# Where the first three chunks of gated activations are split: from PSUM, or after a round trip through DRAM

## The chip, the cores and the metric

The kernel runs on one core of one Trainium2 chip. The metric is the device time of one execution in microseconds (us); lower is better. TensorE is called PE here, VectorE DVE, ScalarE ACT, GpSimd POOL and SyncE SP, as in the profile.

## The reference

One decoder layer on 256 tokens of width 2048. The first half (three attention mixers, their projections, gates and an output projection) is not touched by the change. The second half is a SwiGLU feed-forward layer in float32:

```python
    h2 = rmsnorm(x, g_ffn)
    gu = h2 @ w_gu                                    # 256 x 2048 times 2048 x 11264
    x = x + (jax.nn.silu(gu[..., :D_FF]) * gu[..., D_FF:]) @ w_down   # D_FF = 5632
```

## The kernel before

**Precision.** Every float32 matrix is taken apart into two `fp32r` parts, `hi` (a cast by ACT) and `lo` (source minus `hi`, a subtraction by DVE), by `split` (lines 103 to 107; its two instructions stand at line 105 in the profile). A product is three matmuls, hi·hi, hi·lo and lo·hi (`product`, lines 167 to 169). The left operand, the activations, is loaded as 128x128 weights; the weight matrix streams as 512 columns. So PE needs, for each 128x1024 block of weights that SP fetches, one ACT cast (`w_hi`) and one DVE subtraction (`w_lo`). `w_hi` and `w_lo` have 5 buffers each, the raw blocks 4 to 6.

**The gate and up stage.** A loop over 11 chunks `c` of 512 columns of D_FF. Each turn calls `project_pair`, which computes the gate and the up columns of one chunk together by a Strassen-like scheme (fewer products, more additions on DVE, and two accumulating DMAs on POOL, `u<-g_raw` at line 360). It ends with Silu (ACT, line 947) and a multiplication (DVE, line 948), which leave two 128x512 tiles `sg`, one for each half `t` of the tokens. For the down projection these must be transposed; `to_a` is queued in `stages` and advanced between the weight blocks of the next `project_pair`, so the transposes of chunk `c` run early in the turn of chunk `c+1`.

**`to_a`.** `transpose4` makes four 128x128 transposes on PE (line 189) into one PSUM bank, a `tr` tile (2 buffers). ACT copies it to SBUF (line 938), and POOL issues a DMA that writes it to `a_mem` in DRAM (line 939).

**`take_a`.** It reads a whole chunk back from `a_mem` with a DMA on POOL (line 959) into `a_raw` (2 buffers) and splits it into the chunk's place in the object `a` (tiles `a_hi`, `a_lo`, and others for the chunks in `WD`). For the three chunks 0, 1 and 2 (`ORDER[:EARLY]`) the place is in the pool `pe`, which is free during the gate and up stage; for the other eight it is in `pd`, whose memory is the normed activations `h2` until that stage ends.

**What sets the order.** The program is written once and a scheduler orders each engine's queue by its own estimate of when things become ready. Each engine then runs its queue strictly in that order: an instruction that waits holds up all that stand behind it on its engine. The scheduler put the splits of chunks 0 to 2 into the gate and up stage, one in each of the turns 1, 2 and 3.

Of the kernel before, what the change touches and what calls it, by code (L numbers as in the profile page):

```python
# [27 lines left out]
NF = D_FF // P  # L28
# [26 lines left out]
def hybrid_block(ctx: ExitStack, tc: tile.TileContext, x, g_mix, w_in, q_gain, k_gain, w_branch, w_out,  # L55
# [22 lines left out]
    def pool(stack, name, side, bufs=1):  # L78
        return stack.enter_context(tc.tile_pool(name=name, bufs=bufs, side=side, reuse_waits="tile"))
# [8 lines left out]
    def half_kb(dt=F32):  # L88

        return scratch.tile([P, NB], dt, name="sc")  # L90
# [13 lines left out]
    def split(hi, lo, src, pin=False):  # L104
        for op in nc.scalar.copy(hi, src), nc.vector.tensor_sub(lo, src, hi.bitcast(F32)):  # L105
            if pin:
                tc.keep_in_program_order(op)
# [77 lines left out]
    def transpose4(src):  # L185

        pt = tr.tile([P, 4, P], F32, name="tr")
        for i in range(4):
            nc.tensor.transpose(pt[:, i, :], src[:, i * P:(i + 1) * P], ident)  # L189
        return pt  # L190
# [696 lines left out]
    pe = pool(ctx, "pe", "left")  # L887
# [43 lines left out]

    a_mem = dram.tile([NF // 4, P, 4, S], F32, name="a_mem")

    def to_a(c, srcs):
        for t in range(NT):
            pt = transpose4(srcs[t])
            st = half_kb().rearrange("p (k q) -> p k q", k=4)
            nc.scalar.copy(st, pt)
            nc.gpsimd.dma_start(a_mem[c, :, :, t * P:(t + 1) * P], st)
            yield  # L940

    for c in range(D_FF // NB):
        nxt = (h2, w_gu, (c + 1) * NB, D_FF + (c + 1) * NB) if c + 1 < D_FF // NB else None
        (g0, g1_, u0, u1), ahead = project_pair(h2, w_gu, c * NB, D_FF + c * NB, ahead, nxt)
        sg = [half_kb() for _ in range(NT)]
        for t, (g, u) in enumerate(((g0, u0), (g1_, u1))):
            nc.scalar.activation(sg[t], g, AF.Silu, scale=rstd2[:, t:t + 1])
            nc.vector.scalar_tensor_tensor(sg[t], u, rstd2[:, t:t + 1], sg[t], op0=ALU.mult, op1=ALU.mult)
        stages.append(to_a(c, sg))

    WD = (4, 6, 8)
    ORDER = [0, 1, 2, 4, 3, 6, 5, 8, 7, 9, 10]
    EARLY = 3
    a = Chunks(None, "a", NF // 4, WD, False)

    def take_a(pl, c):
        a.place(pl, c)
        raw = pr.tile([P, 4, S], F32, name="a_raw", bufs=2)
        nc.gpsimd.dma_start(raw, a_mem[c])
        if c in WD:  # L960
            t0, t1 = (raw[:, :, t * P:(t + 1) * P] for t in range(NT))
            a.put(c, 0, t0)
            a.put(c, 1, t1)
            a.put_sums(c, t0, t1, raw)
        else:
            split(*a.t[c], raw)

    for c in ORDER[:EARLY]:
        take_a(pe, c)
    h2_stack.close()  # L970
    pd = pool(ctx, "pd", "left")

    def take_rest():
        for c in ORDER[EARLY:]:
            take_a(pd, c)
            yield
            yield
# [3 lines left out]
    def down_pair(c0, mine, spare, queues):  # L981
# [25 lines left out]
        def seven(c, f1, f5, f6, f7, last):  # L1007
            def quarter(kh, n):
                return load(w_down, 4 * c + 2 * kh, c0 + n * NB, gd)

            b11 = quarter(0, 0)
            form(f1, 1, c, b11, last)
            yield
            b12 = quarter(0, 1)
            u = gd.tile([P, 2, NB], F32, name="u", bufs=1)
            tc.keep_in_program_order(nc.vector.tensor_add(u, b11, b12))
            form(f5, 5, c, u, last)
            yield
            b22 = quarter(1, 1)
            nc.vector.tensor_add(u, u, b22)  # L1020
            form(f6, 6, c, u, last)
            yield
            nc.vector.tensor_add(b12, b12, b22)
            form(f7, 7, c, b12, last)
            yield
            form(own[0, 1], 3, c, b22)
            yield
            b21 = quarter(1, 0)
            form(own[0, 0], 2, c, b21)
            yield  # L1030
            nc.vector.tensor_add(u, u, b21)
            form(own[1, 0], 4, c, u)
            yield

        def combine(f1, f5, f6, f7):

            s1 = snapshot(f1)
            nc.vector.tensor_add(xc[0, 0], xc[0, 0], s1)
            nc.vector.tensor_add(s1, f6, s1)
            s3 = half_kb()  # L1040
            nc.vector.tensor_add(s3, f7, s1)
            s5 = snapshot(f5)
            yield
            nc.vector.tensor_add(xc[1, 0], xc[1, 0], s3)
            nc.vector.tensor_sub(s1, s5, s1)
            nc.vector.tensor_add(xc[0, 1], xc[0, 1], s1)
            nc.vector.tensor_sub(s3, s5, s3)
            nc.vector.tensor_add(xc[1, 1], xc[1, 1], s3)
            yield

        def by_sevens():
            f = spare()
            for c in WD:
                yield from seven(c, *f, c == WD[-1])
            yield from combine(*f)

        sevens = by_sevens()
        plain = [(c, n, kh) for c in ORDER if c not in WD for kh in range(2) for n in range(2)]
        for i, at in enumerate(plain[:-4]):
# [56 lines left out]
```

## Time and profile before

| | |
|---|---|
| median of 3 runs | 1387.82 us (1387.64 to 1389.24) |
| profiled execution, own time | 1387.56 us |
| span in its profile | 1385.8 us |
| PE busy | 1362.3 us, 98% |
| DVE busy | 1151.7 us, 83% |
| ACT busy | 880.9 us, 64% |
| POOL busy | 109.4 us, 8% |
| mean granted PE clock | 0.994 |
| DMA | 331.07 MB, mean 239 GB/s |

The gate and up stage reaches from about 700 us to 1144 us of the span, the down projection from there to the end. In the rows that follow, "idle before <- releaser" in brackets is how long the engine stood still before an instruction and what came last. `DMA_DIRECT2D` is the issue of a DMA, not its transfer. A number after `x` counts merged instructions. `PEld` is the load of weights on PE. The names `ps`, `qs`, `z` and `v` are the PSUM accumulators, `tr` the transposed tiles, `h_shi` and `h_slo` the summed activations of the scheme.

### The profile page before, as it was taken

What the parts mean: (1) busy time and instruction counts of PE and PEld (TensorE: products, weight loads), DVE (VectorE), ACT (ScalarE), POOL (GpSimd) and SP (SyncE); (2) the same over time, 40 slices, a digit from 0 to 9 for tenths busy, and PEclk for the clock granted to TensorE, in tenths of its full rate; (3) what the DMA queues carried; (4) which work ended last, traced back from release to release, by engine and by line L of the source; (5) the groups of instructions that cost most, each with busy time, mean ns of one, the idle gap of its engine ahead of it and who ended that gap; (6) DMA issues with size and microseconds to landing.
All of it is one profiled execution on the core that took longest, in us unless ns stands there. A gap on an engine that the chain in (4) does not pass through costs nothing.

```text
span 1385.8 us, 17910 instructions
## 1 busy us (share of the span) xinstructions
PE 1362.3 (98%) x6404; PEld 1184.9 (85%) x6404; DVE 1151.7 (83%) x1222; ACT 880.9 (64%) x1140; POOL 109.4 (8%) x173
## 2 busy tenths in 40 slices
PE   9999999999999999999999988999999999999998
PEld 7888888888888888888887877888888888788887
DVE  7888797858989987776698877999999998887785
ACT  7678877767776665445565656667666665564553
POOL 1100000000010112101001001010000010100000
PEclk9999999999999999999999999999999999999999
DMA  8875567576687779877887677678787877767553
GB/s 277 288 255 169 202 181 257 147 242 196 244 286 266 263 228 336 276 220 227 294 276 252 224 244 228 214 259 285 247 277 244 274 216 236 258 239 258 195 178 101
DMA packets 93928, 331.07 MB, mean 239 GB/s; under 512 B 11312, under 2 KB 12928, under 8 KB 93840
## 3 DMA queue, kind: packets, MB, share of 16 engines
q1 hardware_dynamic: 76896, 275.29, 57.1%
q0 software_dynamic: 15760, 53.60, 15.0%
q8 instruction: 50, 0.82, 0.2%
q10 hardware_dynamic: 1184, 1.06, 0.2%
q14 instruction: 38, 0.31, 0.1%
HBM read 292.65 MB, written 16.27 MB: 223 GB/s over the span
## 4 chain that ended last, share of the span: by engine, by line
PE 77%; issue 12%; DMA 4%; ACT 3%; DVE 3%; POOL 1%; POOLq 0%; ACTq 0%; DVEq 0%
PE ps L167 9%; PE ps L168 9%; PE ps L169 9%; PE qs L169 9%; PE qs L168 9%; PE qs L167 9%; PE z L167 4%; PE z L169 4%; PE z L168 4%; DMA a_raw<-a_mem 2%; PE v L167 2%; PE v L168 2%; PE v L169 2%; PE tr L189 1%; ACT w_hi L105 1%
## 5 line engine op out<-in xcount | busy, mean ns | idle before, releaser
L105 DVE TENSOR_TENSOR w_lo<-w_raw,w_hi 128x1024 fp32r<-128x1024 f32 x334 | 405.2, 1221 | 84.7 <-ACT w_hi L105 81.9
L105 ACT CAST w_hi<-w_raw 128x1024 fp32r<-128x1024 f32 x334 | 347.4, 1048 | 177.3 <-PE qs L169 80.1
L105 ACT CAST w_hi<-g_raw 128x1024 fp32r<-128x1024 f32 x184 | 191.5, 1048 | 137.0 <-DVE g_raw L310 45.8
L105 DVE TENSOR_TENSOR w_lo<-g_raw,w_hi 128x1024 fp32r<-128x1024 f32 x184 | 221.3, 1222 | 37.3 <-ACT w_hi L105 34.1
L105 ACT CAST w_hi<-u 128x1024 fp32r<-128x1024 f32 x138 | 143.8, 1047 | 82.9 <-PE qs L169 17.8
L105 DVE TENSOR_TENSOR w_lo<-u,w_hi 128x1024 fp32r<-128x1024 f32 x138 | 167.8, 1221 | 27.4 <-ACT w_hi L105 26.6
L168 PE MATMUL ps<-w_lo,h_hi 128*128 128x512 f32 x360 | 136.7, 380 | 0.0
L169 PE MATMUL ps<-w_hi,h_lo 128*128 128x512 f32 x360 | 136.4, 379 | 0.0
L167 PE MATMUL ps<-w_hi,h_hi 128*128 128x512 f32 x360 | 134.0, 383 | 0.0
L168 PE MATMUL qs<-w_lo,h_hi 128*128 128x512 f32 x332 | 126.4, 381 | 0.0
L169 PE MATMUL qs<-w_hi,h_lo 128*128 128x512 f32 x332 | 125.9, 380 | 0.0
L167 PE MATMUL qs<-w_hi,h_hi 128*128 128x512 f32 x332 | 122.5, 381 | 0.0
L169 PEld LDWEIGHTS ps<-w_hi,h_lo 128*128 128x128 f32 x360 | 68.0, 189 | 9.6
L168 PEld LDWEIGHTS ps<-w_lo,h_hi 128*128 128x128 f32 x360 | 68.1, 189 | 9.3
L167 PEld LDWEIGHTS ps<-w_hi,h_hi 128*128 128x128 f32 x360 | 67.8, 189 | 9.2
L321 DVE TENSOR_TENSOR u<-g_raw 128x1024 f32<-128x1024 f32 x40 | 48.8, 1219 | 26.7 <-DMA g_raw<-in_w_in 18.6
L169 PEld LDWEIGHTS qs<-w_hi,h_lo 128*128 128x128 f32 x332 | 62.8, 189 | 9.4 <-issue 0.6
L168 PEld LDWEIGHTS qs<-w_lo,h_hi 128*128 128x128 f32 x332 | 62.8, 189 | 9.0 <-DVE w_lo L105 0.4
L167 PEld LDWEIGHTS qs<-w_hi,h_hi 128*128 128x128 f32 x332 | 62.7, 189 | 8.6
L167 PE MATMUL v<-w_hi,h_hi 128*128 128x512 f32 x120 | 47.7, 397 | 13.3 <-ACT w_hi L105 13.3
L310 DVE TENSOR_TENSOR u<-u,g_raw 128x1024 f32<-128x1024 f32 x40 | 47.2, 1219 | 0.0
L310 DVE TENSOR_TENSOR g_raw<-g_raw 128x1024 f32<-128x1024 f32 x40 | 47.1, 1218 | 0.0
(398 smaller groups left out, 2950.2 us busy)
## 6 DMA issues: line engine op xcount, KB each, us to landing
w_raw<-in_w_in SPq DMA_DIRECT2D x118, 512.0 KB, 4.7
g_raw<-in_w_gu SPq DMA_DIRECT2D x88, 512.0 KB, 6.1
w_raw<-in_w_gu SPq DMA_DIRECT2D x88, 512.0 KB, 6.6
g_raw<-in_w_in SPq DMA_DIRECT2D x72, 512.0 KB, 6.2
w_raw<-in_w_down SPq DMA_DIRECT2D x64, 512.0 KB, 4.3
u<-g_raw POOLq DMA_DIRECT2D x40, 512.0 KB, 5.5
w_raw<-in_w_branch SPq DMA_DIRECT2D x32, 512.0 KB, 4.8
w_raw<-in_w_out SPq DMA_DIRECT2D x32, 512.0 KB, 4.3
```

The lines of the kernel that those rows point to most:

```text
L105: for op in nc.scalar.copy(hi, src), nc.vector.tensor_sub(lo, src, hi.bitcast(F32)):
L167: nc.tensor.matmul(ps, ah, wh, start=start, stop=False, **how)
L168: nc.tensor.matmul(ps, ah, wl, start=False, stop=False, **how)
L169: nc.tensor.matmul(ps, al, wh, start=False, stop=stop, **how)
L189: nc.tensor.transpose(pt[:, i, :], src[:, i * P:(i + 1) * P], ident)
L310: tc.keep_in_program_order(nc.vector.tensor_add(d, d, a))
L321: nc.vector.tensor_add(d, a, b)
```

## The change

Chunks 0, 1 and 2 get their place in `pe` before the gate and up loop. Their transposes are split directly from PSUM: `to_a` calls `a.put(c, t, pt)`, a cast by ACT and a subtraction by DVE for each half `t`, into half of the columns of `a_hi` and `a_lo`. They are no longer copied to SBUF, written to `a_mem`, read back, or split from `a_raw`. The other eight chunks go the old way.

```diff
+    WD = (4, 6, 8)
+    ORDER = [0, 1, 2, 4, 3, 6, 5, 8, 7, 9, 10]
+    EARLY = 3
+    a = Chunks(None, "a", NF // 4, WD, False)
+
+    for c in ORDER[:EARLY]:
+        a.place(pe, c)
+
     def to_a(c, srcs):
         for t in range(NT):
             pt = transpose4(srcs[t])
+            if c in ORDER[:EARLY]:
+                a.put(c, t, pt)
+                yield
+                continue
             st = half_kb().rearrange("p (k q) -> p k q", k=4)
             nc.scalar.copy(st, pt)
             nc.gpsimd.dma_start(a_mem[c, :, :, t * P:(t + 1) * P], st)
...
-    WD = (4, 6, 8)
-    ORDER = [0, 1, 2, 4, 3, 6, 5, 8, 7, 9, 10]
-    EARLY = 3
-    a = Chunks(None, "a", NF // 4, WD, False)
...
-    for c in ORDER[:EARLY]:
-        take_a(pe, c)
```

The order of the queues before and after, at three places, with the tiles' numbers. First ACT in the turn of chunk 1, where chunk 0 is transposed (`w_hi` is the cast of a weight block, `sc` a scratch tile, `a_hi0` the place of chunk 0); before:

```order
L938 COPY sc_6723<-tr_6718 128x512
L938 COPY sc_6741<-tr_6736 128x512
L105 CAST w_hi_6794<-u_6660 128x1024
L305 COPY sc_6750<-z_6686 128x512
L105 CAST w_hi_6804<-u_6661 128x1024
L105 CAST w_hi_6820<-w_raw_6818 128x1024
L105 CAST w_hi_6838<-g_raw_6648 128x1024
L105 CAST a_hi0_10162<-a_raw_10164 128x1024
L105 CAST w_hi_6848<-g_raw_6650 128x1024
L105 CAST w_hi_6862<-w_raw_6860 128x1024
```

and after:

```order
L105 CAST a_hi0_6314<-tr_6724 128x4x128
L105 CAST a_hi0_6314<-tr_6741 128x4x128
L105 CAST w_hi_6798<-u_6666 128x1024
L305 COPY sc_6754<-z_6692 128x512
L105 CAST w_hi_6808<-u_6667 128x1024
L105 CAST w_hi_6824<-w_raw_6822 128x1024
L105 CAST w_hi_6842<-g_raw_6654 128x1024
L105 CAST w_hi_6852<-g_raw_6656 128x1024
L105 CAST w_hi_6866<-w_raw_6864 128x1024
```

The two copies out of PSUM became two casts at the same place, and the cast from `a_raw` that stood between the two casts from `g_raw` is gone. On DVE in the same turn, before:

```order
L310 TENSOR_TENSOR u_6660<-u_6660,g_raw_6756 128x1024
L310 TENSOR_TENSOR u_6661<-u_6661,g_raw_6758 128x1024
L105 TENSOR_TENSOR w_lo_6795<-u_6660,w_hi_6794 128x1024
L105 TENSOR_TENSOR w_lo_6805<-u_6661,w_hi_6804 128x1024
L105 TENSOR_TENSOR w_lo_6821<-w_raw_6818,w_hi_6820 128x1024
L310 TENSOR_TENSOR g_raw_6648<-g_raw_6648,g_raw_6756 128x1024
L310 TENSOR_TENSOR g_raw_6650<-g_raw_6650,g_raw_6758 128x1024
L105 TENSOR_TENSOR w_lo_6839<-g_raw_6648,w_hi_6838 128x1024
L105 TENSOR_TENSOR a_lo0_10163<-a_raw_10164,a_hi0_10162 128x1024
L105 TENSOR_TENSOR w_lo_6849<-g_raw_6650,w_hi_6848 128x1024
```

and after:

```order
L310 TENSOR_TENSOR u_6666<-u_6666,g_raw_6760 128x1024
L310 TENSOR_TENSOR u_6667<-u_6667,g_raw_6762 128x1024
L105 TENSOR_TENSOR a_lo0_6315<-tr_6724,a_hi0_6314 128x4x128
L105 TENSOR_TENSOR a_lo0_6315<-tr_6741,a_hi0_6314 128x4x128
L105 TENSOR_TENSOR w_lo_6799<-u_6666,w_hi_6798 128x1024
L105 TENSOR_TENSOR w_lo_6809<-u_6667,w_hi_6808 128x1024
L105 TENSOR_TENSOR w_lo_6825<-w_raw_6822,w_hi_6824 128x1024
L310 TENSOR_TENSOR g_raw_6654<-g_raw_6654,g_raw_6760 128x1024
L310 TENSOR_TENSOR g_raw_6656<-g_raw_6656,g_raw_6762 128x1024
L105 TENSOR_TENSOR w_lo_6843<-g_raw_6654,w_hi_6842 128x1024
```

The one subtraction from `a_raw` became two half-size subtractions from `tr`, six rows further up, between the additions into `u` and the subtractions `w_lo<-u`. On POOL from the accumulations into `u` of chunk 0 on, before:

```order
L360 DMA u_6282<-g_raw_6287 128x1024
L939 DMA a_mem_6313<-sc_6723 512x1x128
L939 DMA a_mem_6313<-sc_6741 512x1x128
L360 DMA u_6660<-g_raw_6664 128x1024
L959 DMA a_raw_10164<-a_mem_6313 128x1024
L360 DMA u_6661<-g_raw_6666 128x1024
L939 DMA a_mem_6313<-sc_7074 512x1x128
L939 DMA a_mem_6313<-sc_7092 512x1x128
```

and after, the first writes and reads that are left (those of chunk 3, and the reads of chunks 4 and 3):

```order
L951 DMA a_mem_6313<-sc_7776 512x1x128
L951 DMA a_mem_6313<-sc_7794 512x1x128
L360 DMA u_7713<-g_raw_7717 128x1024
L360 DMA u_7714<-g_raw_7719 128x1024
L951 DMA a_mem_6313<-sc_8127 512x1x128
L951 DMA a_mem_6313<-sc_8145 512x1x128
L360 DMA u_8064<-g_raw_8068 128x1024
L966 DMA a_raw_10243<-a_mem_6313 128x1024
L966 DMA a_raw_10293<-a_mem_6313 128x1024
L360 DMA u_8065<-g_raw_8070 128x1024
```

Six writes and three reads left the queue; in the turn of chunk 1 the second accumulation into `u` no longer has a read of `a_mem` in front of it, and the reads of chunks 4 and 3 stand in the turn where they stood. The queue of SP has the same instructions in the same order, and PE's differs in the place of one matmul.

## The prediction

> **What bounds the kernel now.** I read the page first, then who PE waited for, then the gate and up stage period by period, then the instructions around one wait. The page says that PE is the bound:
>
> ```profile
> span 1385.8 us, 17910 instructions
> PE 1362.3 (98%) x6404; PEld 1184.9 (85%) x6404; DVE 1151.7 (83%) x1222; ACT 880.9 (64%) x1140; POOL 109.4 (8%) x173
> ```
>
> PE is idle for 1385.8 - 1362.3 = 23.5 us in all, and the change leaves PE's own work as it is: only these 23.5 us, and time in which PE was busy but slow, can move. The waits of PE over the whole span, the two longest, and then waits of all engines between 640 and 900 us (total, times, longest):
>
> ```profile
> PE v L167 <- ACT w_hi L105: 13.3, 4, 4.2
> PE tr L387 <- DVE sc L405: 1.5, 1, 1.5
> ```
>
> ```profile
> ACT a_hi L105 <- DMA a_raw<-a_mem: 14.1, 3, 4.8
> PE v L167 <- ACT w_hi L105: 12.6, 3, 4.2
> POOL a_raw L959 <- DMA a_mem<-sc: 4.8, 2, 2.5
> ```
>
> One kind of wait makes up more than half of PE's idle time: three times about 4.2 us, for a `w_hi` of ACT; and ACT in the same stretch waited three times for the read of `a_raw` from DRAM. Three is the number of chunks that the change takes off that way. I cut the stage into periods, from the first copy of one chunk's transposes on ACT to that of the next (columns: length; busy time and count of PE, PEld, DVE, ACT, POOL; granted clock; DMA share; GB/s):
>
> ```profile
> 746.72:793.50 46.78, 42.60 (x189) 36.59 (x188) 38.13 (x36) 27.50 (x31) 3.83 (x5) 0.93 0.69 225
> 793.50:839.13 45.63, 41.39 (x189) 35.75 (x188) 37.78 (x36) 27.51 (x32) 3.83 (x5) 0.96 0.70 230
> 839.13:885.80 46.67, 42.47 (x189) 36.51 (x188) 37.91 (x36) 27.50 (x31) 3.84 (x5) 0.93 0.69 226
> 885.80:925.53 39.73, 39.73 (x189) 34.83 (x188) 36.61 (x35) 26.68 (x31) 3.29 (x4) 1.00 0.76 252
> 925.53:965.25 39.72, 39.72 (x189) 34.83 (x188) 36.49 (x35) 26.68 (x30) 4.43 (x6) 1.00 0.84 278
> ```
>
> The same 189 PE instructions take 39.73 us in a period without a split from `a_raw`, with PE never idle and the clock at 1.00, and 45.63 to 46.78 us in the three with one. Inside the second period, by engine:
>
> ```profile
> 794.38 1.59 POOL L939 DMA_DIRECT2D a_mem<-sc  x2 [38.51 <-ACT sc L938]
> 800.80 0.56 POOL L959 DMA_DIRECT2D a_raw<-a_mem  x1 [2.29 <-DMA a_mem<-sc]
> 806.81 1.04 ACT L105 CAST a_hi<-a_raw 128x1024 fp32r<-128x1024 f32 x1 [4.80 <-DMA a_raw<-a_mem]
> 808.71 1.04 ACT L105 CAST w_hi<-w_raw 128x1024 fp32r<-128x1024 f32 x1
> 805.18 0.38 PE L169 MATMUL z<-w_hi,h_lo 128*128 128x512 f32 x1
> 809.80 0.80 PE L167 MATMUL v<-w_hi,h_hi 128*128 128x512 f32 x1 [4.24 <-ACT w_hi L105]
> ```
>
> So the chain is: transposes copied, written to DRAM, the read issued at 800.80 once the write has landed, its data there at 806.8. ACT stands 4.80 us in front of the cast from `a_raw`; the weight cast that PE needs next is queued behind it, ends at 808.71 + 1.04 = 809.75, and PE starts 0.05 us later.
>
> **The change, part by part.** *The wait goes.* PE would have gone on one matmul after the last. First the pitch of matmuls (a window of the same stage without a pause), then the last matmul ahead of the gap, the first behind it and the first that is fast again, for the other two periods, then the last of these for the second:
>
> ```profile
> 1100.00:1120.00 20.00, 20.00 (x94) 17.52 (x93) 17.71 (x18) 12.23 (x14) 0.00 (x0) 1.00 0.79 303
> ...
> 758.40 0.38 PE L169 MATMUL z<-w_hi,h_lo 128*128 128x512 f32 x1
> 762.95 0.79 PE L167 MATMUL v<-w_hi,h_hi 128*128 128x512 f32 x1 [4.18 <-ACT w_hi L105]
> 768.48 0.38 PE L169 MATMUL ps<-w_hi,h_slo 128*128 128x512 f32 x1
> 850.81 0.38 PE L169 MATMUL z<-w_hi,h_lo 128*128 128x512 f32 x1
> 855.39 0.80 PE L167 MATMUL v<-w_hi,h_hi 128*128 128x512 f32 x1 [4.21 <-ACT w_hi L105]
> 860.56 0.38 PE L168 MATMUL ps<-w_lo,h_shi 128*128 128x512 f32 x1
> 812.80 0.38 PE L169 MATMUL qs<-w_hi,h_slo 128*128 128x512 f32 x1
> ```
>
> The pitch is 20.00 / 94 = 0.21 to 0.22 us. The starts are late by 762.95 - 758.40 - 0.22 = 4.33, 809.80 - 805.18 - 0.22 = 4.40 and 855.39 - 850.81 - 0.22 = 4.36 us, 13.09 together. The rest of the loss is the clock: PE resumes at about half pace and is back at full pace after 5.5, 3.0 and 5.2 us. Both are in the length of the periods, which I take for the sum: (46.78 + 45.63 + 46.67) - 3 x 39.73 = 139.08 - 119.19 = 19.89 us. The clock's part is thus 19.89 - 13.09 = 6.80 us. No gap, no drop: the period of 39.73 us has neither.
>
> [...]
>
> *ACT.* The rows of the added and the removed instructions; the gate stage has no split from PSUM yet, but the transposes of the merged activations earlier in the kernel are split in the same way (same tile, same output layout):
>
> ```profile
> L938 ACT COPY sc<-tr x22: 576/590/597, 746.7 to 1168.2; 128x512 f32<-128x512 f32 x22
> L105 ACT CAST m_hi<-tr x8: 586/592/600, 553.7 to 618.9; 128x512 fp32r<-128x512 f32 x8
> L105 ACT CAST a_hi<-a_raw x3: 1044/1044/1044, 760.0 to 852.4; 128x1024 fp32r<-128x1024 f32 x3
> L105 DVE TENSOR_TENSOR a_lo<-a_raw,a_hi x3: 1225/1226/1226, 761.0 to 853.5; 128x1024 fp32r<-128x1024 f32 x3
> 619.59 1.28 DVE L105 TENSOR_TENSOR m_lo<-tr,m_hi 128x512 fp32r<-128x512 f32 x2
> ```
>
> Six copies of 0.59 become six casts of 0.59 at the same place: nothing. Three casts of 1.04 go: 3.1 us less, worth nothing beyond the wait, since ACT is idle for a third of each period.
>
> *DVE.* Three subtractions of 1.23 go (3.7 us), six come, 1.28 a pair (3.8 us). The total hardly moves, but the pair now stands early, in front of what PE needs soon. DVE is busy 36.61 of 39.73 us in a free period, so 1.28 more fits; the question is how late the weights become on the way. The undisturbed period after chunk 3 shows the slack (the last two rows are PE's loads ahead of the matmuls that need the two ACT results above them):
>
> ```profile
> 885.80 1.25 ACT L938 COPY sc<-tr 128x512 f32<-128x512 f32 x2 [1.36 <-PE tr L189]
> 885.84 2.36 DVE L310 TENSOR_TENSOR u<-u,g_raw 128x1024 f32<-128x1024 f32 x2
> 889.66 1.22 DVE L105 TENSOR_TENSOR w_lo<-u,w_hi 128x1024 fp32r<-128x1024 f32 x1 [0.20 <-ACT w_hi L105]
> 891.94 2.35 DVE L310 TENSOR_TENSOR g_raw<-g_raw 128x1024 f32<-128x1024 f32 x2
> 893.27 2.18 ACT L105 CAST w_hi<-g_raw 128x1024 fp32r<-128x1024 f32 x2 [2.69 <-DVE g_raw L310]
> 895.36 1.05 ACT L105 CAST w_hi<-w_raw 128x1024 fp32r<-128x1024 f32 x1
> 896.31 0.57 ACT L305 COPY sc<-qs 128x512 f32<-128x512 f32 x1
> 897.48 0.19 PEld L167 LDWEIGHTS v<-w_hi,h_hi 128*128 128x128 f32 x1
> 897.92 0.19 PEld L167 LDWEIGHTS qs<-w_hi,h_shi 128*128 128x128 f32 x1
> ```
>
> The pair goes in at 885.84 + 2.36 = 888.20 and lasts until 889.48. The first `w_lo<-u` follows, and the second, one such pitch (2.35 - 1.22 = 1.13) later, starts at 890.6 instead of 889.66: its wait of 0.20 is gone, and what follows comes about 0.9 us later, the additions on `g_raw` and through them ACT's casts behind the 2.69 us wait. The cast for `v` would end at 896.41 + 0.9 = 897.3 against 897.48, the snapshot of `qs` at 896.88 + 0.9 = 897.8 against 897.92. Slack of 0.1 to 0.2 us is left; the first period starts some 0.2 us behind this one, so I put down 0.1 us for all three. Ends: 0 if the slack holds, 3 x 1.28 = 3.8 us if none of it covers. It is nearest to 0, because each row has its slack, and DVE has 39.73 - 36.61 = 3.1 us of idle time per period in which to catch up.
>
> *POOL and DMA.* Six issues (1.59 a pair) and three (0.56) go: 6.5 us of an engine that is 8% busy, nothing. The second accumulation into `u` in these turns no longer stands behind the read, which waited 2.29 us; it comes earlier, and no wait of PE for it shows. Six transfers of 0.25 MB out and three of 0.5 MB back go, 3 MB in all of 331: nothing but relief. The reads of chunks 4 and 3 stay in their turn, and the period in which they are issued (925.53:965.25) shows no idle PE, since they are split only after the stage. The rest of the down projection has its order unchanged. SP's queue is unchanged; its loads come earlier as the buffers come free earlier.
>
> *Sum.* 1387.56 (the profiled execution: span 1385.8 and 1.76 around it) - 19.89 + 0.1 = 1367.8 us. The median of the runs is 0.26 above that execution, so I say **1367.9 us**. What PE waits for next are single waits below 2 us at the start, at the beginning of the down projection and at the end.
>
> **The rivals.** *DVE's pair reaches PE.* The slack above is as short as 0.1 us. If the pair costs between half and all of itself in each turn, 1.9 to 3.8 us come back: 1369.8 to 1371.7 us. For it: DVE is the second busiest engine, 92% in a free period. Against: the working above. I add no half clock to it: of the periods shown only those with the gap of over 4 us are below 1.00. Chance 0.14.
>
> *Another wait takes the place.* While ACT stood still, weight loads ran ahead. Without the pause each turn might end in a wait for a load, which I bound by half of the pause: 3 x 2.2 = 6.5 us back, 1374.4 us. For it: DMA is at 0.84 in the period 925.53:965.25. Against: the two turns shown that have no such pause run at 39.73 and 39.72 without a wait, the second of them behind one that had none either. Chance 0.04.
>
> *The wait is not from the round trip,* PE would have waited for the weights all the same: no change, 1387.8 us. Against: PE restarts 0.05 us after the cast that stood behind the one from `a_raw`. Chance 0.02.
>
> *Slower: DVE waits in front of the pair.* Before, DVE never waited for the transposes; now its queue stands until ACT has cast both halves, and ACT until PE has transposed. If DVE arrives early there, `w_lo` and with it PE stand still in a ring of waits. In the free period ACT starts on the transposes at 885.80 and is done at 887.05, DVE arrives at 888.20, over 1 us later. The deciding point is a loss of (19.89 + 2.8) / 3 = 7.6 us a turn, more than the pause that goes; the time would be above 1390.6 us. Chance 0.02.
>
> **How the numbers follow.** The forecast, the whole gain with up to 1 us back, has 0.78: 1366.8 to 1368.8 us with the spread of the runs (0.2 below, 1.4 above their median) around it. Range 1366.3 to 1371.7 us: the low end takes 1.5 us for a disturbed run of before in the base and for relief elsewhere, the high end the whole of DVE's pair. It leaves out the last three cases. A change of 0.2%, 2.8 us, is about what can be told from none here; the first three cases are beyond it: faster 0.96, same 0.02, slower 0.02.
>
> **What would show it.** Right: the three periods at 39.7 to 40.1 us with clock 1.00; no PE wait for `w_hi` above 0.5 us between 740 and 870; PE idle about 11 us over the span; DVE's `a_lo<-tr` near 0.68 each, with no wait of DVE in front of them. Wrong: a period above 41 us, with PE waiting for `w_hi` or `w_lo` behind the pair, or for a load; or a new wait in the down projection.

## The result, and the profile after

| | before | after |
|---|---|---|
| median | 1387.73 us (1386.44 to 1389.24, 4 runs) | 1366.64 us (1366.02 to 1367.05, 4 runs) |
| ratio, 95% interval | | 0.9847 (0.983 to 0.9864) |
| span of the profiled execution | 1385.8 us | 1364.9 us |

The kernel is 21.1 us faster between medians, 20.9 between the two spans; 19.8 were forecast, and the time came 1.3 us below the forecast, inside its range. One execution of a kernel below, that with four copies, took 2918.47 us with the clock at 1.00 and is left out of that kernel's figures. From the page after, the span and the busy times, and from the view of waits the longest of PE over the whole span (total, times, longest):

```profile
span 1364.9 us, 17884 instructions
PE 1354.4 (99%) x6404; PEld 1180.6 (86%) x6404; DVE 1149.7 (84%) x1225; ACT 878.0 (64%) x1137; POOL 103.0 (8%) x164
```

```profile
PE tr L387 <- DVE sc L405: 1.5, 1, 1.5
PE ps L167 <- ACT w_hi L105: 0.9, 2, 0.5
PE tr L673 <- ACT kT L745: 0.8, 1, 0.8
PE v L167 <- ACT w_hi L105: 0.7, 1, 0.7
```

PE is idle for 1364.9 - 1354.4 = 10.5 us instead of 23.5, and the row with 13.3 us in four waits has shrunk to one of 0.7. The 1.5 us that now lead stood in the view of waits before too. The gate and up stage cut in the same way, from the ACT instruction that takes one chunk's transposes out of PSUM to the next (length; busy time and count of PE, PEld, DVE, ACT, POOL; granted clock; DMA share; GB/s):

```profile
745.93:785.65 39.72, 39.72 (x189) 34.82 (x188) 37.53 (x37) 26.48 (x30) 1.72 (x2) 1.00 0.74 239
785.65:825.38 39.73, 39.73 (x189) 34.82 (x188) 37.26 (x37) 26.56 (x30) 1.71 (x2) 1.00 0.75 238
825.38:865.11 39.73, 39.73 (x189) 34.83 (x188) 37.26 (x37) 26.57 (x30) 1.71 (x2) 1.00 0.73 239
865.11:904.84 39.73, 39.73 (x189) 34.82 (x188) 36.67 (x35) 26.68 (x31) 3.30 (x4) 1.00 0.78 252
```

The three periods that took 139.08 us now take 119.18, with PE never idle and the clock at 1.00, the same as the undisturbed fourth. That is 19.90 us, and it is nearly the whole result: 0.79 us lie ahead of the first transposes (746.72 before, 745.93 after) and 1385.8 - 885.80 - (1364.9 - 865.11) = 0.2 us behind the third period.

### The profile page after: what moved, and what is told of

Read it like the earlier page. It is cut to its first block, busy times and chain, and to the rows that moved or that the text cites. A ratio compares the mean times of both kernels' runs of the same rounds, so it can differ in the third digit from the quotient of the medians.

```text
span 1364.9 us, 17884 instructions
## 1 busy us (share of the span) xinstructions
PE 1354.4 (99%) x6404; PEld 1180.6 (86%) x6404; DVE 1149.7 (84%) x1225; ACT 878.0 (64%) x1137; POOL 103.0 (8%) x164
## 5 line engine op out<-in xcount | busy, mean ns | idle before, releaser
L360 POOL DMA_DIRECT2D u<-g_raw x40 | 35.1, 878 | 232.1 <-DVE w_lo L105 175.8
```

The source lines that it names most:

```text
L360: nc.gpsimd.dma_start(d, a, accum_op=ALU.add)
```

## The experiments

The kernels of one group ran on one chip beside runs of the kernel before, whose medians were 1388.46, 1388.10 and 1388.31 us. Unless stated otherwise, each kernel is the changed one with the edit shown. The questions: was it the round trip through DRAM that cost the time, or only where it stood in ACT's queue? Is PE's gap the whole price? And how near is DVE's new pair to becoming the next wait?

**The round trip kept, its split later in the turn.** This one is the kernel before, edited: a chunk's split is queued further down the same turn.

```diff
+        if c in ORDER[:EARLY]:            # in to_a, behind both halves; take_a for these is gone
+            raw = pr.tile([P, 4, S], F32, name="a_raw", bufs=2)
+            nc.gpsimd.dma_start(raw, a_mem[c])
+            for _ in range(12):
+                yield
+            split(*a.t[c], raw, pin=True)
+            yield
```

> The kernel before, with the round trip through DRAM kept for all three chunks (two writes, one read, one split from a_raw each), but the split put some 18 us further down in the same turn, when the read has long landed. If the loss was ACT standing in its queue in front of a cast whose data was not there, this is as fast as the changed kernel: 1366.6 us, at most 1 us above it for the later place of DVE's 1.23 us subtraction, and periods of 39.7 us with clock 1.00. If the round trip itself costs (DMA traffic, the issues on POOL, the longer way), it stays above 1380 us.

Measured 1367.00 us (1366.33 to 1367.92, 5 runs), ratio 0.9849 (0.9835 to 0.9862). First the windows of the first two turns, then ACT in the first around the split from `a_raw`:

```profile
745.80:785.52 39.72, 39.72 (x189) 34.83 (x188) 37.71 (x36) 27.32 (x31) 3.83 (x5) 1.00 0.78 265
785.52:825.25 39.73, 39.73 (x189) 34.83 (x188) 37.52 (x36) 27.41 (x31) 3.83 (x5) 1.00 0.80 265
```

```profile
763.07 1.05 ACT L105 CAST w_hi<-u 128x1024 fp32r<-128x1024 f32 x1 [0.62 <-PE z L169]
764.03 1.04 ACT L105 CAST a_hi<-a_raw 128x1024 fp32r<-128x1024 f32 x1
764.97 1.04 ACT L105 CAST w_hi<-u 128x1024 fp32r<-128x1024 f32 x1
```

All six writes, three reads, copies and full-size splits are still there (POOL is busy 3.83 us a turn, as before), and the whole gain is made. ACT now reaches the cast 764.03 - 745.80 = 18.2 us after the transposes, when its data have landed, and waits for nothing; before it came there after 806.81 - 4.80 - 793.50 = 8.5 us and stood. So the way through DRAM cost at most 0.4 us by itself (a median of 1367.00 us against the 1366.64 of the change); what cost the time was a cast standing in ACT's queue ahead of its data, for 4.80 us in that turn of before.

**The change, with its old traffic added again.** The split halves are also written to `a_mem` and read back into `a_raw`, where nobody uses them.

```diff
                 a.put(c, t, pt)
+                nc.gpsimd.dma_start(a_mem[c, :, :, t * P:(t + 1) * P], a.t[c][0][:, :, t * P:(t + 1) * P].bitcast(F32))
                 yield
+                if t:
+                    raw = pr.tile([P, 4, S], F32, name="a_raw", bufs=2)
+                    nc.gpsimd.dma_start(raw, a_mem[c])
                 continue
```

> The changed kernel, plus the traffic that it took away: each of the three chunks is written from its a_hi to a_mem and read back into a_raw, and nothing uses what is read. ACT and DVE work is that of the changed kernel. If traffic and POOL's issues cost nothing: 1366.6 us, within 0.5. If the relief of DMA and POOL was a part of the gain (also of the 1 us that came on top of the forecast): 1367.6 us or more, up to 1387.

Measured 1367.77 us (1366.94 to 1368.85, 4 runs), ratio 0.9854 (0.9841 to 0.9868): 1.1 us above the change, with each ratio inside the other's interval. By the number alone this is the second branch of the expectation, 1367.6 us or more. In its profile, though, the turns with the traffic take no longer than those of the change; the windows of the first two:

```profile
745.94:785.66 39.72, 39.72 (x189) 34.82 (x188) 37.47 (x37) 26.37 (x30) 3.85 (x5) 1.00 0.81 265
785.66:825.39 39.73, 39.73 (x189) 34.83 (x188) 37.16 (x37) 26.60 (x30) 3.85 (x5) 1.00 0.78 265
```

From the stage on, the profile first differs at 1163 us, in the down projection, in single waits of 0.2 to 0.8 us for weights, long after the added transfers. A cost of the traffic is not shown by this, and the 1.1 us stay unexplained; the kernel with the later split, which has the same transfers, is at 1367.00 us.

**Only chunk 0 direct**; chunks 1 and 2 go by way of DRAM.

```diff
-            if c in ORDER[:EARLY]:
+            if c == 0:
                 a.put(c, t, pt)
...
+    for c in ORDER[1:EARLY]:
+        take_a(None, c)
```

> The changed kernel with only chunk 0 split from PSUM; chunks 1 and 2 go by way of DRAM as before. If each chunk's wait is a loss of its own, the first period falls to 39.7 us and the other two stay at 45.6 to 46.8: 1387.7 - 7 = 1380.7 us, between 1380 and 1382. If the waits hang together (a pause gives the loads time and shields the next turn), the other two periods change too and the time is outside that.

Measured 1380.67 us (1380.28 to 1381.9, 4 runs), ratio 0.9948 (0.9935 to 0.9962). The windows of its three turns:

```profile
745.22:784.95 39.73, 39.73 (x189) 34.82 (x188) 37.56 (x37) 26.48 (x31) 1.72 (x2) 1.00 0.73 239
784.95:832.49 47.54, 43.01 (x189) 36.89 (x188) 37.91 (x36) 27.51 (x31) 3.87 (x5) 0.93 0.66 221
832.49:878.51 46.02, 41.41 (x189) 35.77 (x188) 37.78 (x36) 27.51 (x32) 3.88 (x5) 0.96 0.69 229
```

Each chunk carries its own loss: the turn of the direct chunk is free, the other two lose 7.81 and 6.29 us. These are not the sizes of before, 5.90 and 6.94 us in the same turns. PE's gaps are a little longer, 4.5 and 4.6 us, and the clock of 0.93 now falls to the earlier of the two turns and that of 0.96 to the later, the other way round than before; the last section comes back to that.

**DVE's pair made twice**, to use up the slack of 0.1 to 0.2 us that the prediction saw.

```diff
                 a.put(c, t, pt)
+                hi, lo = (x[:, :, t * P:(t + 1) * P] for x in a.t[c])
+                nc.vector.tensor_sub(lo, pt, hi.bitcast(F32))
                 yield
```

> The changed kernel with DVE's pair of subtractions a_lo<-tr made twice in each of the three turns: 1.28 us more of DVE early in the turn, nothing else. The trace of the changed kernel has 0.08 us of slack between ACT's cast for v and PE's load for it. If that slack is all, PE waits about 1.1 to 1.2 us in each turn: 1366.6 + 3.4 = 1370.0 us, clock 1.00. If DVE's idle 3 us per period cover it: 1366.6 us.

A miss: 1366.27 us (1365.1 to 1366.81, 4 runs), ratio 0.9842 (0.9828 to 0.9855), no slower than the change. First the changed kernel's first turn, then the same rows here:

```profile
748.46 1.28 DVE L105 TENSOR_TENSOR a_lo<-tr,a_hi 128x512 fp32r<-128x512 f32 x2
...
754.39 2.19 ACT L105 CAST w_hi<-g_raw 128x1024 fp32r<-128x1024 f32 x2 [3.46 <-DVE g_raw L310]
756.49 1.04 ACT L105 CAST w_hi<-w_raw 128x1024 fp32r<-128x1024 f32 x1
...
757.61 0.19 PEld L167 LDWEIGHTS v<-w_hi,h_hi 128*128 128x128 f32 x1
...
757.82 0.38 PE L167 MATMUL v<-w_hi,h_hi 128*128 128x512 f32 x1
```

```profile
748.32 1.28 DVE L105 TENSOR_TENSOR a_lo<-tr,a_hi 128x512 fp32r<-128x512 f32 x2
...
750.65 1.28 DVE L948 TENSOR_TENSOR a_lo<-tr,a_hi 128x512 fp32r<-128x512 f32 x2
...
755.45 1.06 ACT L105 CAST w_hi<-g_raw 128x1024 fp32r<-128x1024 f32 x1 [4.66 <-DVE g_raw L310]
...
757.83 1.05 ACT L105 CAST w_hi<-w_raw 128x1024 fp32r<-128x1024 f32 x1
...
757.81 0.19 PEld L168 LDWEIGHTS ps<-w_lo,h_shi 128*128 128x128 f32 x1 [0.15 <-DVE w_lo L105]
...
759.22 0.38 PE L167 MATMUL v<-w_hi,h_hi 128*128 128x512 f32 x1
```

The second pair does delay ACT's casts, by 1.2 us (its wait grows from 3.46 to 4.66). But the scheduler knew of the added work and put seven matmuls of `ps` ahead of `v`; a load for one of them waited 0.15 us. The time is that of the second branch of the expectation, but by the new order and not by DVE's idle time. The periods are 39.75 and 39.74, 0.01 to 0.03 us longer. So the experiment shows that a turn has room for this much more DVE work when the program is ordered for it; it does not show how much delay the order of the changed kernel would have borne.

**ACT made busy instead**, with no round trip for the three chunks: copies in place of a raw weight block ahead of one of its casts, in the turns of chunks 1 to 3. Two, four and six of them, in three kernels.

```diff
                 if f == 7 and i == 1:             # in project_pair
+                    for _ in range(again):        # 2, 4 or 6 if c in (1, 2, 3) else 0
+                        nc.scalar.copy(srcs[i], srcs[i])
```

Two:

> The changed kernel with ACT kept busy where the cast from a_raw stood: two copies of 128x1024 in place, about 2.0 us, ahead of the second cast from g_raw in the three turns. No DMA is added. PE should wait about 2.4 us in each turn (2.0, and a snapshot of 0.5 that now stands in front, less the slack of 0.1). If a gap that short leaves the clock alone: 1366.6 + 7.2 = 1373.8 us. If it brings half a clock as the gaps of 4.2 us did (2.3 us each): 1380.7 us.

Four:

> The same with four copies, about 4.0 us: PE should wait about 4.4 us in each of the three turns, as in the kernel before, with no round trip through DRAM. If the loss before was this gap and the half clock behind it: 1366.6 + 13.2 + 6.8 = 1386.6 us (1385 to 1388), clock below 1.00 in the three periods. If the half clock has another cause than the gap: 1379.8 us.

Six, after the two others were seen:

> The changed kernel with six copies of 128x1024 in place on ACT ahead of one weight cast in each of the three turns, instead of four (nothing else differs, and no transposed chunk goes by way of DRAM). With four, PE stood 1.93 and 0.46 us in a turn and a turn at full clock took 2.92 us longer. Two copies more, 1.07 us each by the rows of four, make the first gap 4.1 us, about the 4.2 us of the kernel before. The theory that a weight cast made late on ACT is the whole price, whatever holds ACT up: 5.1 us a turn at full clock, and with half clock after each gap of 3.4 to 6.8 us (1.7 to 3.4 us lost) 6.8 to 8.5 us a turn, so 1366.5 + 20.4 to 25.5 = 1387 to 1392, at or a little above the kernel before. The rival, that half the loss before belonged to the transposes' way through DRAM and not to PE's gap: no more half clock than with four copies, 1366.5 + 3 x 5.1 + at most 3.4 = 1382 to 1385.

| copies | median (range, runs) | ratio, 95% interval | the three periods, us |
|---|---|---|---|
| 2 | 1368.70 us (1368.19 to 1369.12, 4) | 0.9863 (0.9849 to 0.9876) | 40.50, 40.50, 40.50 |
| 4 | 1379.23 us (1377.98 to 1379.4, 3) | 0.9936 (0.9921 to 0.9951) | 42.65, 44.12, 44.12 |
| 6 | 1386.99 us (1386.32 to 1389.67, 10) | 0.9994 (0.9984 to 1.0003) | 46.35, 46.95, 47.37 |

The first two expectations missed: they named gaps of about 2.4 and 4.4 us a turn; the gaps were 0.5 and 2.2 to 2.4, since here too the scheduler put other matmuls ahead. That the time with four copies lies near the 1379.8 us of the second branch is chance, for the clock did fall, in two turns, with gaps half as long as assumed. With six copies the first gap came out as expected, and the time at the low end of the 1387 to 1392 us of the theory, clear of the rival's 1382 to 1385; the rows of PE at the first gap and the windows of the three turns:

```profile
763.01 0.48 PE L167 MATMUL ps<-w_hi,h_shi 128*128 128x512 f32 x1 [4.08 <-ACT w_hi L105]
763.96 0.80 PE L167 MATMUL v<-w_hi,h_hi 128*128 128x512 f32 x1 [0.46 <-ACT w_hi L105]
```

```profile
745.58:791.93 46.35, 41.81 (x189) 35.85 (x188) 37.55 (x37) 32.64 (x36) 1.72 (x2) 0.96 0.64 204
791.93:838.88 46.95, 42.94 (x189) 36.53 (x188) 37.62 (x37) 32.64 (x36) 1.71 (x2) 0.93 0.60 202
838.88:886.25 47.37, 43.36 (x189) 36.83 (x188) 37.62 (x37) 32.64 (x37) 1.71 (x2) 0.93 0.60 200
```

With four copies:

```profile
745.42:788.07 42.65, 40.26 (x189) 34.72 (x188) 37.38 (x37) 30.34 (x34) 1.72 (x2) 1.00 0.67 222
788.07:832.19 44.12, 41.95 (x189) 35.88 (x188) 37.40 (x37) 30.55 (x34) 1.71 (x2) 0.96 0.66 215
832.19:876.31 44.12, 41.95 (x189) 35.93 (x188) 37.39 (x37) 30.44 (x34) 1.71 (x2) 0.96 0.67 215
```

With first gaps of 3.9 to 4.1 us the old time is back (140.67 us for the three turns, 139.08 before), half clock included, though no early chunk goes through DRAM. What costs is a weight cast that comes late on ACT, whether a wait for DRAM or other work on ACT makes it late.

**The change again, and with chunk 10 direct as well.** Chunk 10 is the last to be transposed; its place is in `pd`, which opens at the start of the down projection. The second kernel splits it from PSUM there.

```diff
-            if c in ORDER[:EARLY]:
+            if c in ORDER[:EARLY] or c == ORDER[-1]:
...
+    a.place(pd, ORDER[-1])
...
-        for c in ORDER[EARLY:]:
+        for c in ORDER[EARLY:-1]:
```

The change again:

> The changed kernel again, on this chip: 1366.6 us, within 0.7. If the 0.8 us that it gained ahead of the first transposes comes from the run and not from the code, the first of them may start anywhere between 745.9 and 746.7 us; if from the code, at 745.9 again.

And with chunk 10:

> The changed kernel with the last chunk (10) split from PSUM too, at the beginning of the down projection; seven chunks go by way of DRAM. ACT and DVE there split the same amount, one write and one read are gone. The waits of PE in that stretch are 2 us in all. If the chain of reads through the two a_raw buffers causes them, up to 2 us are gained: 1364.6 to 1366.0 us. If the amount of splitting on ACT and DVE in that stretch causes them: 1366.6 us, within 0.5.

The change measured 1366.44 us (1365.06 to 1366.78, 5 runs), ratio 0.9845 (0.9832 to 0.9859); with chunk 10 direct 1363.28 us (1362.06 to 1364.06, 4 runs), ratio 0.9823 (0.981 to 0.9836), another 3.2 us less and more than the 2 that were allowed for. The profile of the change at this place, three casts of ACT and three waits of PE:

```profile
1177.01 1.04 ACT L105 CAST a_hi<-a_raw 128x1024 fp32r<-128x1024 f32 x1 [7.05 <-DMA a_raw<-a_mem]
1177.96 1.04 ACT L105 CAST w_hi<-u 128x1024 fp32r<-128x1024 f32 x1
1178.91 1.04 ACT L105 CAST w_hi<-w_raw 128x1024 fp32r<-128x1024 f32 x1
...
1179.05 0.48 PE L167 MATMUL ps<-w_hi,a_1hi 128*128 128x512 f32 x1 [0.48 <-ACT w_hi L105]
1180.00 0.70 PE L167 MATMUL qs<-w_hi,a_hi 128*128 128x512 f32 x2 [0.46 <-ACT w_hi L105]
...
1189.59 0.48 PE L168 MATMUL v<-w_lo,a_shi 128*128 128x512 f32 x1 [0.60 <-DVE w_lo L105]
```

A window of the change around it (length, then busy time and count of PE first):

```profile
1150.00:1200.00 50.00, 47.94 (x216) 39.91 (x215) 44.71 (x46) 29.58 (x32) 4.72 (x9) 1.00 0.74 241
```

With chunk 10 direct, the same three casts of ACT and the same window:

```profile
1170.37 1.05 ACT L105 CAST w_hi<-u 128x1024 fp32r<-128x1024 f32 x1 [1.32 <-PE ps L169]
1171.67 1.05 ACT L105 CAST w_hi<-w_raw 128x1024 fp32r<-128x1024 f32 x1 [0.24 <-PE qs L169]
...
1176.54 1.04 ACT L105 CAST a_hi<-a_raw 128x1024 fp32r<-128x1024 f32 x1 [3.82 <-DMA a_raw<-a_mem]
```

```profile
1150.00:1200.00 50.00, 49.54 (x229) 42.75 (x228) 47.00 (x48) 30.87 (x33) 3.71 (x7) 1.00 0.73 243
```

It is the same pattern at a second place: ACT stands 7.05 us in front of a cast from `a_raw`, two weight casts are queued behind it, and PE waits for both. With chunk 10 direct the two weight casts stand ahead of the cast from `a_raw`, ACT stands only 3.82 us in front of it, and the three waits are gone; a fourth of 0.46 us, at 1193.95 us in the change, stays (1190.22 here). 13 matmuls more fit into the window, 13 x 0.213 = 2.8 us; the three waits are 1.54 of that. ACT and DVE split the same amount, so that is not the cause. But the first branch of the expectation, a shorter chain of reads, is not shown either: the read for this cast is issued at 1170.33 us (1169.78 in the change), and the cast starts only 0.47 us earlier. What changed in front of PE is the order of ACT's queue, which the scheduler made anew for this kernel; no run moves the casts alone at this place.

## Why the prediction was right

**The wait and the clock (-19.89 us).** Measured -19.90 in the three periods. The steps of the argument hold separately: the place in ACT's queue is the cause (the round trip kept and split later gives the full gain), the loss is per chunk (only chunk 0 direct), and a late cast on ACT is enough to make it (six copies). Taking the period and not the gap alone was what mattered: the gaps were 13.09 of it, the clock 6.80. The traces' record of the granted clock bears out that share: half clock for 6.83, 3.41 and 6.83 us in the kernel before, 13.2 us of it after PE had resumed, and half of that is 6.6.

**ACT (0).** The six casts from PSUM stand in the place of the copies and take the same time, and DVE's six subtractions the 0.68 us each that the prediction named:

```profile
L105 ACT CAST a_hi<-tr x6: 587/590/593, 745.9 to 826.0; 128x512 fp32r<-128x512 f32 x6
L105 DVE TENSOR_TENSOR a_lo<-tr,a_hi x6: 681/682/684, 748.5 to 828.3; 128x512 fp32r<-128x512 f32 x6
```

**DVE (+0.1 us).** The pair of 1.28 us went in where the working put it, with no wait in front, and ACT's casts behind the wait for `g_raw` came 754.39 - 745.93 = 8.46 us after the start of the first period, against 893.27 - 885.80 = 7.47 in the free period of before: 0.99 us later, and 0.78 in the next two, where 0.9 was expected. The cast for `v` ended at 756.49 + 1.04 = 757.53 and PE loaded at 757.61: a slack of 0.08 us (0.31 in the next two turns), and no wait. The forecast of 0.1 came out as 0, with little to spare in the first turn. The rival in which DVE's pair reaches PE was priced as if PE's order were fixed; the kernel with two pairs shows that this order gives way when the scheduler knows the cost.

**POOL, DMA (0).** Confirmed for the three turns by the two kernels that keep the traffic, whose turns run at 39.72 and 39.73 us; the 1.1 us that one of them takes longer elsewhere are open.

**The size.** 1.3 us more came than was forecast for the median. In the profiled executions 0.8 of it lies ahead of the first transposes, where the two kernels have the same work in the same order. Nearly all of that arises at 718 us: there PE waits 0.33 and 0.29 us in the kernel before, 0.16 us once in the change, and not at all in the profile of the change taken again. The first transposes start at 745.0 to 745.9 us in all ten profiles after the change and its variants (745.93 and 745.34 in the two of the change itself), and at 746.72 in the one profile of before. Whether the kernel before always starts later is not settled with one profile. No term of the sum stands for this part, only the low end of the range leaves room for it, so it came by luck. The interval of the ratio, 18.9 to 23.6 us, holds the forecast gain of 19.8.

## What to carry to other kernels

Look for an instruction that waits for a DMA in the queue of an engine that also feeds PE: here it cost not its own duration (1.04 us) but the wait of everything queued behind it (4.2 us of PE a turn), and moving it down the queue until its data had landed was worth as much as removing the transfer (1367.00 against 1366.64 us). Price such a wait by the length of the whole period against an undisturbed one: here the clock's drop came on top of the gap, 6.80 of 19.89 us. Where a scheduler orders the program, an experiment that adds work can also change the order (two copies made a gap of 0.5 us where 2.4 were expected), so read the gap it really made, and the order of the queue, before using its time.

## What the runs showed of the hardware

The half clock came behind gaps much shorter than the 4.18 to 4.24 us of the kernel before, too. With four copies PE stood only 1.71 us and then 0.46 us, with one matmul between, in the turn shown, and the drop came in two of three turns, after PE had resumed. PE in the second turn, then two windows there (PE's busy time stands behind the length, the clock ahead of the last two numbers):

```profile
803.13 0.48 PE L167 MATMUL qs<-w_hi,h_shi 128*128 128x512 f32 x1 [1.71 <-ACT w_hi L105]
804.08 0.48 PE L167 MATMUL v<-w_hi,h_hi 128*128 128x512 f32 x1 [0.46 <-ACT w_hi L105]
...
805.01 0.63 PE L169 MATMUL qs<-w_hi,h_slo 128*128 128x512 f32 x1
```

```profile
801.00:804.40 3.40, 1.23 (x5) 0.51 (x4) 1.29 (x2) 3.37 (x4) 0.00 (x0) 1.00 0.17 52
804.40:807.80 3.40, 3.40 (x10) 2.71 (x9) 3.40 (x4) 3.31 (x5) 0.00 (x0) 0.53 0.35 86
```

The matmuls at 803.13 and 804.08 take 0.48 us, as the one behind the first gap with six copies does; those behind 804.6 are slow for some 3.4 us (0.63 us against the 0.38 of an undisturbed one). In the 3.4 us ahead of the drop PE was busy for 1.23 us, so here a drop followed a stretch that was a third busy. In the first turn of the same kernel, gaps of 1.93 and 0.46 us brought no drop.

So the length of a gap does not tell these turns apart. Where the gap falls does, as far as the record of the granted clock shows. Windows of the kernel before, cut at the changes of the clock: the 3.41 us ahead of each drop and the 3.41 us behind it, and the stretches at full clock between the slow ones:

```profile
758.04:761.45 3.41, 0.73 (x4) 0.30 (x2) 0.41 (x1) 1.49 (x2) 0.00 (x0) 1.00 0.85 183
761.45:764.86 3.41, 1.91 (x5) 1.55 (x6) 3.41 (x4) 3.41 (x5) 0.00 (x0) 0.50 0.02 4
768.28:809.24 40.96, 37.28 (x177) 32.35 (x175) 33.06 (x32) 23.57 (x27) 3.83 (x5) 1.00 0.70 236
805.83:809.24 3.41, 0.00 (x0) 0.00 (x0) 1.35 (x2) 2.43 (x3) 0.00 (x0) 1.00 0.59 123
809.24:812.65 3.41, 2.85 (x7) 2.30 (x8) 3.41 (x4) 2.89 (x4) 0.00 (x0) 0.50 0.17 16
812.65:853.61 40.96, 38.54 (x183) 33.44 (x181) 33.15 (x32) 23.40 (x27) 3.84 (x5) 1.00 0.77 255
850.20:853.61 3.41, 0.99 (x5) 0.53 (x3) 0.13 (x1) 1.21 (x2) 0.00 (x0) 1.00 0.84 181
853.61:857.02 3.41, 1.63 (x4) 1.36 (x5) 3.41 (x4) 3.41 (x5) 0.00 (x0) 0.50 0.02 5
```

The half-clock stretches are 3.41 or 6.83 us long, and 40.96 us, 12 x 3.413, lie from the end of one to the start of the next. Counted off in steps of 3.41 us from the changes of the clock, the steps that ended in a drop in these turns had PE busy for 21, 0 and 29% of the time in the kernel before, 36 and 38% with four copies, and 0 to 18% in the other kernels with drops. The first turn with four copies spreads its two gaps over steps of 56 and 74%. No step of 56% or more at full clock is followed by a drop in any of the eleven profiles; what lies between 38 and 56% none of these turns shows.

By the same count, two of the three slow stretches of the kernel before were longer than the third where PE was busy for less of their first step. The clock fell while PE still stood, at 761.45, 809.24 and 853.61 us, so it was busy for only 56, 83 and 48% of the first half-clock step; after the 83% the clock was back, after the other two a second step followed. How busy a step has to be is not settled: with six copies one of 89% did not bring the clock back, and one of 93% did. So gaps of nearly the same length, 4.2 to 4.6 us, cost 5.9 to 7.8 us a turn, with slow stretches of 3.41 or 6.83 us, which this count puts down to where the gaps fall.
